# First weights by row block, squares a block late, and the memory rows' sums moved behind the index projections

## The chip, the core and the metric

The kernel runs on one NeuronCore of one Trainium2 chip. A core has five engines that run side by side, each through its own queue of instructions in a fixed order: TensorE (PE, matrix products; its weight loads are shown as PEld), VectorE (DVE), ScalarE (ACT), GpSimd (POOL) and SyncE (SP, which here issues the transfers between the chip's memory and the core's buffer). An instruction starts when it is at the head of its queue and what it waits for is done. The metric is the device time of one execution in microseconds; lower is better.

## What is computed

A decoder trunk of two layers over 512 tokens of width 1024, with five attention branches that share one normalised input, one of them attending to 256 memory rows. What matters here is the first projections of a layer and the memory branch:

```python
def _rmsnorm(x, g):
    xf = x.astype(jnp.float32)
    y = xf * lax.rsqrt(jnp.mean(xf * xf, axis=-1, keepdims=True) + EPS)
    return (y * g.astype(jnp.float32)).astype(x.dtype)

def _layer(x, mem, ...):
    h = _rmsnorm(x, norm_g)
    p = _split_columns(h @ w_in)
    ...
    y_c = _stick_breaking_attention(heads(p['sb_q']), heads(p['sb_k']), heads(p['sb_v']))
    ...
    mkv = _rmsnorm(mem, mem_norm) @ w_mem_kv
    mem_k = mkv[..., :BR_WIDTH].reshape(B, -1, N_HEADS, HEAD_DIM)
    mem_v = mkv[..., BR_WIDTH:].reshape(B, -1, N_HEADS, HEAD_DIM)
    y_e = _memory_attention(heads(p['mem_q']), mem_k, mem_v)
    ...
    return x + merged @ w_out
```

## The kernel before, in words

**Tiles.** Activations lie transposed: 1024 channels are 8 row blocks of 128 partitions, with 512 tokens along the free axis. Every float32 operand of a large product is split in two: a high part (ACT copies it into the rounded type) and a low part (DVE subtracts the high part from the original). `mm3` makes three products of each pair of blocks: high by high, low input by high weight, high input by low weight. A projection of 128 output columns (`proj`) is 8 row blocks times 3 = 24 matmuls.

**Weights.** `load` brings 128 x 1024 values (512 KB) through SP into one of two raw buffers (tag "raw", two of them), `split` turns them into `whi` and `wlo` (three buffers each). A raw buffer is free again when its low part is done, so SP's next weight transfer stands behind that. The memory rows (`mem_proj`, tile `mraw`) use the same two raw buffers.

**The start of layer 0.** `first` makes the projection of the first queries and keys (`sb_q`, `sb_k`, heads 0 and 1) from x that is multiplied by the norm's gain only; the row scale (root of the mean square) is applied to the results. `begin_tile` makes for each row block the high part `uh` (ACT), the square `sq` (ACT), the low part `ul` (DVE) and the running sum of squares (DVE). `inorder` writes the order on ACT and DVE out by hand: each instruction of the start stands behind the one before. The first weights come in two halves, one for each of the two output tiles (`START_W`), and are split behind row blocks 1 and 3. Then `sumsq` (PE adds the squares over channels), `rsqrt4` (twelve small steps on DVE, tiles `rs_v` to `rs_y`), `rotary_tables` (tile `ang`, then sine and cosine on ACT), the values of the first branch (`sb_v`), `rowb` (PE spreads the row scale over the partitions), and `norm`, which makes the normalised input `h_hi`, `h_lo` for all later projections.

**Behind it.** `memory_rows` makes the same root for the 256 memory rows: squares on ACT, sums on DVE (tile `sq`), the sum over channels on PE (`ssq`), the root on DVE, `rowb` on PE, and the result `rmem`. `sb_pair(1)` projects the second pair of queries and keys, `small_proj` the small heads and the index queries (`v2`, `iq`), `sb_attn` is the stick-breaking attention (tiles `sbz`, `sp_t`, `sp`, `sb_a`, and `Yc`, its product with the values). `mem_proj` scales the memory rows by `rmem` and the gain (`mraw`), splits them (`yhi`, `ylo`) and projects keys (`memk`, two tiles of 24 matmuls on 256 rows) and values (`memv`, 48).

**What sets the order.** A scheduler orders each engine's queue when the program is built, from the order of the code and the priorities; `weave` draws steps from generators in fixed shares, `chain` runs generators one behind the other, `take(g, n)` takes n steps, and `early` raises the priority of loads and splits.

Of the kernel before, what the change touches and what calls it, by code (L numbers as in the profile page):

```python
# [103 lines left out]
def _layout(x, mem, positions, norm_g, w_in, kv_norm, w_uk, w_uv, fox_bias, nsa_pe_k, nsa_pe_v,  # L104
# [6 lines left out]
    for l in range(L):  # L111
# [8 lines left out]
        for a, b in PAIRS:  # L120
            wall[l, CH[a]].reshape(128, 2, KT, 128)[:, 0] = cols(tl[a])
            wall[l, CH[a]].reshape(128, 2, KT, 128)[:, 1] = cols(tl[b])
# [64 lines left out]
def trunk(ctx: ExitStack, tc: tile.TileContext, xt, memt, pos, wall, small, vec, ca, cb, out):  # L187
# [27 lines left out]
    nc.scalar.preload_act_table_set("exp_and_others")  # L215
# [4 lines left out]
    START_W = (1, 3)  # L220
    start_w = []
    for k in range(KT):
        nc.sync.dma_start(xs[:, k], xt[:, k])
        if k in START_W:
            r = wts.tile([128, 1024], F32, name="wraw", tag="raw", bufs=2)
            nc.sync.dma_start(r, wall[0, CH[('sb_q', 0)], :, 1024 * len(start_w):1024 * len(start_w) + 1024])
            start_w.append(r)
# [147 lines left out]
    def memory_rows():  # L375
        rmem = const.tile([128, NM], F32, name="rmem")
        memp = [slot("memx", shape=(128, 2, NM)) for _ in range(4)]
        for j in range(4):
            nc.sync.dma_start(memp[j], memt[:, 2 * j:2 * j + 2])
        y = rsqrt4(sumsq([squares([memp[k // 2][:, k % 2] for k in range(KT)])], 2), D, 2)  # L380
        nc.scalar.activation(rmem, rowb(y, 2)[:, :NM], AF.Copy)
        tabs.rmem = rmem
        yield
# [288 lines left out]
    def begin_layer(l):  # L672

        U = [wk.tile([128, 2, T], F32R, name="u", tag=t, bufs=2) for t in ("yhi", "yhi", "ylo", "ylo", "Z", "Z")]
        u = [x[:, e] for x in U for e in range(2)]
        return SimpleNamespace(uh=u[:KT], ul=u[KT:] + [slot("ul", F32R) for _ in range(2 * KT - len(u))], sq=[])

    def begin_tile(b, l, k, x, inorder=lambda e, ins: ins, middle=lambda k: None):

        sq = slot("sq")  # L680
        g = vcol(l * V_L + V_NG + k)
        inorder(0, nc.scalar.activation(b.uh[k], x, AF.Copy, scale=g))
        middle(k)
        inorder(0, nc.scalar.activation(sq, x, AF.Square))
        inorder(1, nc.vector.scalar_tensor_tensor(b.ul[k], x, g, f32(b.uh[k]), op0=OP.mult, op1=OP.subtract))
        if k == 0 or (l and k == KT - 1):
            b.sq.append(sq)
        else:
            inorder(1, nc.vector.tensor_add(b.sq[0], b.sq[0], sq))

    def layer(l, xs, begin):
# [3 lines left out]
        def first():  # L695
# [4 lines left out]
            if l == 0:  # L700
# [5 lines left out]

                def start_split(k):
                    if k in START_W:
                        w = [wts.tile([128, 1024], F32R, name="w", tag=t, bufs=3) for t in ("whi", "wlo")]
                        r = start_w[START_W.index(k)]  # L710
                        inorder(0, nc.scalar.activation(w[0], r, AF.Copy))
                        inorder(1, nc.vector.tensor_sub(w[1], r, f32(w[0])))
                        ws.append(w)

                for k in range(KT):
                    begin_tile(b, 0, k, xs[:, k], inorder, start_split)
                state['start'] = prev[0], prev[1]
# [3 lines left out]
            for k in range(KT):  # L721
                for a in range(2):
                    c = slice(128 * k, 128 * k + 128)
                    mm3(p[a], ws[a][0][:, c], ws[a][1][:, c], uh[k], ul[k], k == 0, k == KT - 1)
# [661 lines left out]
        if l == 0:  # L1386
            run(chain(memory_rows(), take(sp1, 1)))
# [3 lines left out]
            weave((sb_attn(0), 8), (chain(silu2('sb_z', lv.ZC), take(ixp, 1), take(sp1, 1), take(ixp, 1), mp), 10))  # L1391
# [50 lines left out]
```

## Time and profile before

| | us |
|---|---|
| time, median of 3 executions | 1329.99 (1329.08 to 1330.47) |
| the profiled execution: time | 1330.9 |
| the profiled execution: span | 1329.1 |
| PE busy in the span | 1296.8 |
| DVE busy | 914.0 |
| ACT busy | 674.4 |
| first matmul starts | 9.31 |

The span reaches from the first to the last instruction of the profiled execution; 1.8 us lie around it. Busy time is what an engine spent in instructions; PE's ends are modelled, so a busy PE is not always at its peak rate. In the lists below "idle before <-X" names what ended the engine's wait.

### The profile page before, as it was taken

What the parts mean: (1) busy time and instruction counts of PE and PEld (TensorE: products, weight loads), DVE (VectorE), ACT (ScalarE), POOL (GpSimd) and SP (SyncE); (2) the same over time, 40 slices, a digit from 0 to 9 for tenths busy, and PEclk for the clock granted to TensorE, in tenths of its full rate; (3) what the DMA queues carried; (4) which work ended last, traced back from release to release, by engine and by line L of the source; (5) the groups of instructions that cost most, each with busy time, mean ns of one, the idle gap of its engine ahead of it and who ended that gap; (6) DMA issues with size and microseconds to landing.
All of it is one profiled execution on the core that took longest, in us unless ns stands there. A gap on an engine that the chain in (4) does not pass through costs nothing.

```text
span 1329.1 us, 18893 instructions
## 1 busy us (share of the span) xinstructions
PE 1296.8 (98%) x7160; PEld 1063.7 (80%) x7160; DVE 914.0 (69%) x1981; ACT 674.4 (51%) x1260; POOL 41.8 (3%) x60
## 2 busy tenths in 40 slices
PE   7999999999999999999999999999999999999997
PEld 6777777878888888888887777778788878888896
DVE  6887999768755546555567699995696564564554
ACT  6886835256545434334447695533574453343341
POOL 0000011000000000000000001110000000000000
PEclk9999999999999999999999999999999999999999
DMA  6432231312222222133523223222122222223231
GB/s 220 140 127 69 91 111 64 96 64 75 72 79 88 79 81 78 50 111 129 180 88 127 96 64 128 80 64 95 48 88 64 87 80 80 86 73 111 95 112 64
DMA packets 40235, 124.10 MB, mean 93 GB/s; under 512 B 4432, under 2 KB 6480, under 8 KB 40144
## 3 DMA queue, kind: packets, MB, share of 16 engines
q1 hardware_dynamic: 40144, 122.89, 28.6%
q8 instruction: 56, 0.92, 0.3%
q14 instruction: 35, 0.29, 0.1%
HBM read 118.16 MB, written 4.72 MB: 92 GB/s over the span
## 4 chain that ended last, share of the span: by engine, by line
PE 70%; DVE 6%; ACT 5%; issue 2%; DMA 1%; POOL 0%; DVEq 0%; ACTq 0%
PE pj L259 58%; PE Y L259 4%; PE S L259 3%; PE pt L556 3%; ACT whi L269 1%; DVE wlo L270 1%; DVE score L911 1%; DVE m L910 1%; DMA mraw<-in_memt_dram 1%; PE sbz L259 0%; ACT sw L431 0%; ACT sw L430 0%; ACT sp_t L388 0%; ACT Qi L854 0%; DVE rt L435 0%
## 5 line engine op out<-in xcount | busy, mean ns | idle before, releaser
L259 PE MATMUL pj<-h_hi,whi 128*128 128x512 f32 x1088 | 430.4, 397 | 1.3 <-DVE rt L433 1.0
L259 PE MATMUL pj<-h_lo,whi 128*128 128x512 f32 x1088 | 428.8, 394 | 0.0
L259 PE MATMUL pj<-h_hi,wlo 128*128 128x512 f32 x1088 | 427.9, 393 | 0.0
L269 ACT ACTIVATE whi<-wraw 128x1024 fp32r<-128x1024 f32 x183 | 193.4, 1057 | 347.1 <-PE pj L259 182.3
L270 DVE TENSOR_TENSOR wlo<-wraw,whi 128x1024 fp32r<-128x1024 f32 x183 | 223.6, 1223 | 197.8 <-ACT whi L269 178.7
L259 PEld LDWEIGHTS pj<-h_hi,wlo 128*128 128x128 f32 x1088 | 204.4, 188 | 44.5 <-DVE wlo L270 2.8
L259 PEld LDWEIGHTS pj<-h_hi,whi 128*128 128x128 f32 x1088 | 204.5, 188 | 43.5 <-issue 2.3
L259 PEld LDWEIGHTS pj<-h_lo,whi 128*128 128x128 f32 x1088 | 204.6, 188 | 41.6 <-issue 2.8
L547 ACT ACTIVATE P<-P,nm 128x128 f32<-128x128 f32 (+3 forms) x128 | 71.5, 559 | 55.5 <-DVE nm L546 54.7
L259 PE MATMUL pj<-yhi,whi 128*128 128x512 f32 (+1 forms) x192 | 72.2, 376 | 0.8 <-ACT whi L269 0.6
L259 PE MATMUL pj<-yhi,wlo 128*128 128x512 f32 (+1 forms) x192 | 71.6, 373 | 0.0
L259 PE MATMUL pj<-ylo,whi 128*128 128x512 f32 (+1 forms) x192 | 71.5, 373 | 0.0
L546 DVE CUSTOM_DVE_ANT_0 P<-S,CA 128x128 f32<-128x128 f32 (+3 forms) x104 | 48.0, 466 | 33.6 <-PE S L259 33.6
L556 PE MATMUL pt<-CA,P 128*128 128x128 f32 x384 | 60.7, 274 | 0.7 <-DVE P L595 0.5
L556 PEld LDWEIGHTS pt<-CA,P 128*128 128x128 f32 x384 | 45.6, 141 | 11.1 <-issue 3.6
L394 ACT ACTIVATE G<-pj 128x512 f32<-128x512 f32 x92 | 53.7, 583 | 0.3
L259 PE MATMUL S<-Ks,Qs 128*128 128x256 f32 (+2 forms) x160 | 50.0, 352 | 2.0 <-DVE nm L546 1.8
L911 DVE MATCH_REPLACE8 score<-m,score 128x256 f32<-128x256 f32 (+2 forms) x96 | 51.5, 541 | 0.0
L910 DVE MAX8 m<-score 128x8 f32<-128x256 f32 (+2 forms) x96 | 49.8, 547 | 0.0
L806 DVE TENSOR_TENSOR acc<-acc,G 128x512 f32<-128x512 f32 x64 | 44.0, 687 | 0.8
L805 DVE SCALAR_TENSOR_TENSOR G<-G,pj 128x512 f32<-128x512 f32 x64 | 43.6, 681 | 0.5 <-PE pj L259 0.2
L259 PEld LDWEIGHTS pj<-yhi,whi 128*128 128x128 f32 x192 | 36.1, 188 | 8.3 <-ACT whi L269 0.9
(326 smaller groups left out, 2028.5 us busy)
## 6 DMA issues: line engine op xcount, KB each, us to landing
wraw<-in_wall_dram SPq DMA_DIRECT2D x192, 512.0 KB, 3.7
wc<-in_wall_dram SPq DMA_DIRECT2D x16, 256.0 KB, 5.9
x<-in_xt_dram SPq DMA_DIRECT2D x8, 256.0 KB, 6.2
mraw<-in_memt_dram SPq DMA_DIRECT2D x4, 512.0 KB, 4.7
xo<-in_xt_dram SPq DMA_DIRECT2D x8, 256.0 KB, 3.8
xspill<-xn SPq DMA_DIRECT2D x8, 256.0 KB, 2.3
xo<-xspill SPq DMA_DIRECT2D x8, 256.0 KB, 3.2
out_dram<-o SPq DMA_DIRECT2D x8, 256.0 KB, 2.2
```

The source lines that it names most:

```text
L259: return nc.tensor.matmul(out_, lhsT, rhs, start=start, stop=stop, **kw)
L269: nc.scalar.activation(hi, raw, AF.Copy)
L270: nc.vector.tensor_sub(lo, raw, hi.bitcast(F32))
L394: i = nc.scalar.activation(*a, **k)
L546: nc.vector.tensor_tensor_reduce(P, S, mask, -1.0, 3e38, OP.add, OP.min, nm)
L547: nc.scalar.activation(P, P, AF.Exp, bias=nm, scale=-1.0, accum_out=sums)
L556: nc.tensor.transpose(pt[:, 128 * j:128 * j + 128], x[:, c:c + 128], ident)
L805: nc.vector.scalar_tensor_tensor(G, G, gc, p, op0=gop, op1=OP.mult)
L806: nc.vector.tensor_add(acc, acc, G)
L910: nc.vector.max(m8, lv.work[i])
L911: nc.vector.match_replace(lv.work[i], m8, lv.work[i], REPL)
```

## The change

**The start.** In layer 0 the weights of the first projection are laid out by row block: for each of the 8 row blocks the 128 columns of the queries and the 128 of the keys stand side by side. They are loaded in four pieces of two row blocks (128 x 512 values, 256 KB), the first one from ACT's queue ahead of its table load, the other three from SP's queue, each ahead of the two blocks of x that it belongs to. They are split piece by piece, ahead of the high part of every second row block. The squares run one row block late (`late_square`): behind the high and low part of block k stands the square of block k - 1. The projection's matmuls take their weights from the new places in both layers.

**The memory rows.** `memory_rows` yields behind the squares. Its first part stands behind the second queries instead of ahead of them; its second part (sum, root, `rmem`) stands in the long chain directly ahead of `mem_proj`.

```diff
@@ layout of the weights
+            w2 = wall[l, CH[a]].reshape(128, 2, KT, 128)
+            if a == ('sb_q', 0):
+                w2 = wall[l, CH[a]].reshape(128, KT, 2, 128).transpose(0, 2, 1, 3)
@@ loads of the start
-    nc.scalar.preload_act_table_set("exp_and_others")
...
-    START_W = (1, 3)
-    start_w = []
-    for k in range(KT):
-        nc.sync.dma_start(xs[:, k], xt[:, k])
-        if k in START_W:
-            r = wts.tile([128, 1024], F32, name="wraw", tag="raw", bufs=2)
-            nc.sync.dma_start(r, wall[0, CH[('sb_q', 0)], :, 1024 * len(start_w):1024 * len(start_w) + 1024])
-            start_w.append(r)
+    start_w = [wts.tile([128, 1024], F32, name="wraw", tag="raw", bufs=2) for _ in range(2)]
+
+    def start_load(k):
+        c = slice(512 * (k % 4) // 2, 512 * (k % 4) // 2 + 512)
+        nc.scalar.dma_start(start_w[k // 4][:, c], wall[0, CH[('sb_q', 0)], :, 256 * k:256 * k + 512])
+
+    start_load(0)
+    nc.sync.dma_start(xs[:, 0], xt[:, 0])
+    nc.sync.dma_start(xs[:, 1], xt[:, 1])
+    nc.scalar.preload_act_table_set("exp_and_others")
+    for k in range(2, KT, 2):
+        c = slice(512 * (k % 4) // 2, 512 * (k % 4) // 2 + 512)
+        nc.sync.dma_start(start_w[k // 4][:, c], wall[0, CH[('sb_q', 0)], :, 256 * k:256 * k + 512])
+        for e in range(2):
+            nc.sync.dma_start(xs[:, k + e], xt[:, k + e])
@@ memory_rows
-        y = rsqrt4(sumsq([squares([memp[k // 2][:, k % 2] for k in range(KT)])], 2), D, 2)
+        sq = squares([memp[k // 2][:, k % 2] for k in range(KT)])
+        yield
+        y = rsqrt4(sumsq([sq], 2), D, 2)
@@ begin_tile
+        middle(k)
         inorder(0, nc.scalar.activation(b.uh[k], x, AF.Copy, scale=g))
-        middle(k)
+        inorder(1, nc.vector.scalar_tensor_tensor(b.ul[k], x, g, f32(b.uh[k]), op0=OP.mult, op1=OP.subtract))
+        if l == 0:
+
+            b.rest.append((x, sq))
+            if k:
+                late_square(b, inorder)
+            return
         inorder(0, nc.scalar.activation(sq, x, AF.Square))
-        inorder(1, nc.vector.scalar_tensor_tensor(b.ul[k], x, g, f32(b.uh[k]), op0=OP.mult, op1=OP.subtract))
...
+    def late_square(b, inorder):
+        x, sq = b.rest.pop(0)
+        inorder(0, nc.scalar.activation(sq, x, AF.Square))
+        if b.sq:
+            inorder(1, nc.vector.tensor_add(b.sq[0], b.sq[0], sq))
+        else:
+            b.sq.append(sq)
@@ first
+                ws += [[wts.tile([128, 1024], F32R, name="w", tag=t, bufs=3) for t in ("whi", "wlo")] for _ in range(2)]
+
                 def start_split(k):
-                    if k in START_W:
-                        w = [wts.tile([128, 1024], F32R, name="w", tag=t, bufs=3) for t in ("whi", "wlo")]
-                        r = start_w[START_W.index(k)]
-                        inorder(0, nc.scalar.activation(w[0], r, AF.Copy))
-                        inorder(1, nc.vector.tensor_sub(w[1], r, f32(w[0])))
-                        ws.append(w)
+                    if k % 2 == 0:
+                        c = slice(256 * (k % 4), 256 * (k % 4) + 512)
+                        hi, lo = (x[:, c] for x in ws[k // 4])
+                        r = start_w[k // 4][:, c]
+                        inorder(0, nc.scalar.activation(hi, r, AF.Copy))
+                        inorder(1, nc.vector.tensor_sub(lo, r, f32(hi)))
...
-                    c = slice(128 * k, 128 * k + 128)
-                    mm3(p[a], ws[a][0][:, c], ws[a][1][:, c], uh[k], ul[k], k == 0, k == KT - 1)
+                    c = slice(256 * (k % 4) + 128 * a, 256 * (k % 4) + 128 * a + 128)
+                    mm3(p[a], ws[k // 4][0][:, c], ws[k // 4][1][:, c], uh[k], ul[k], k == 0, k == KT - 1)
@@ the body of layer
-            run(chain(memory_rows(), take(sp1, 1)))
+            mr = memory_rows()
+            run(chain(take(sp1, 1), take(mr, 1)))
...
-            weave((sb_attn(0), 8), (chain(silu2('sb_z', lv.ZC), take(ixp, 1), take(sp1, 1), take(ixp, 1), mp), 10))
+            weave((sb_attn(0), 8), (chain(silu2('sb_z', lv.ZC), take(ixp, 1), take(sp1, 1), take(ixp, 1), mr, mp), 10))
```

How the queues change is shown at three places. The first is DVE's queue at the start; before, its first rows were (`u<-x_79,VEC,u` is a low part of x, `w<-wraw,w` that of the weights, `sq<-sq` a sum of squares):

```order
L685 SCALAR_TENSOR_TENSOR u<-x_79,VEC,u 128x512
L712 TENSOR_TENSOR w<-wraw,w 128x1024
L685 SCALAR_TENSOR_TENSOR u<-x_79,VEC,u 128x512
L689 TENSOR_TENSOR sq<-sq 128x512
L685 SCALAR_TENSOR_TENSOR u<-x_79,VEC,u 128x512
L689 TENSOR_TENSOR sq<-sq 128x512
L712 TENSOR_TENSOR w<-wraw,w 128x1024
```

The weights' low parts stood between low parts of x, in two pieces. Now the same place on DVE reads:

```order
L741 TENSOR_TENSOR w<-wraw,w 128x512
L696 SCALAR_TENSOR_TENSOR u<-x_78,VEC,u 128x512 x2
L741 TENSOR_TENSOR w<-wraw,w 128x512
L696 SCALAR_TENSOR_TENSOR u<-x_78,VEC,u 128x512
L713 TENSOR_TENSOR sq<-sq 128x512
L696 SCALAR_TENSOR_TENSOR u<-x_78,VEC,u 128x512
L713 TENSOR_TENSOR sq<-sq 128x512
L741 TENSOR_TENSOR w<-wraw,w 128x512
```

A quarter of the weights stands ahead of each two blocks of x, and the sums begin behind the third low part. The second place is PE's queue behind the index queries' projection, whose last matmul is the first row here. Before (`smt_p` and `sw_p` belong to the small heads, `pj<-yhi,whi` is the first matmul of the memory keys):

```order
L259 MATMUL pj<-h_hi,wlo 128x512
L829 MATMUL smt_p<-CA,v_684 128x128 x4
L259 MATMUL sw_p<-v_684,CA 128x512
L259 MATMUL sbz<-Qs,Ks 128x256 x2
L259 LDWEIGHTS identb
L259 MATMUL sbz<-sbm,identb 128x256
L259 MATMUL sbz<-sp,nones 128x256 x4
L259 MATMUL sbz<-sp,nones 128x384 x2
L259 MATMUL sbz<-sp,ntri 128x512 x2
L259 MATMUL pj<-yhi,whi 128x256
```

The sum over the memory rows' channels (`ssq<-ones`) and the broadcast of their root (`rowb<-CA,rs_y`) had been done far ahead of this. Now PE's queue reads, from the last stick-breaking row of that piece on:

```order
L269 MATMUL sbz<-sp,ntri 128x512 x2
L269 MATMUL ssq<-ones_100,sq 128x1 x2
L269 MATMUL sbz<-Qs,Ks 128x384 x2
L269 LDWEIGHTS identb
L269 MATMUL sbz<-sbm,identb 128x128
L269 MATMUL sbz<-sp,ntri 128x256 x2
L269 MATMUL sbz<-Qs,Ks 128x256 x2
L269 LDWEIGHTS identb
L269 MATMUL sbz<-sbm,identb 128x256
L327 MATMUL rowb<-CA,rs_y 128x128 x2
```

Sum and broadcast came into this place, with stick-breaking products of the second head between them; the first matmul of the memory keys stands 13 rows behind the broadcast, and only stick-breaking rows are in between. The third place is SP's queue of transfers around the memory rows. Before (`memx` are the memory rows for the squares, `mraw` for the projection, `wraw` weights):

```order
L278 DMA wraw<-in_wall_dram 128x1024
L379 DMA memx<-in_memt_dram 128x512 x2
L1225 DMA mraw<-in_memt_dram 128x1024 x2
L251 DMA cbs<-in_cb_dram 128x512
L819 DMA cosI<-rot 128x1x512
L819 DMA sinI<-rot 128x1x512
L278 DMA wraw<-in_wall_dram 128x1024 x16
```

Two more `memx` stood ahead of the first row here. Now on SP:

```order
L288 DMA wraw<-in_wall_dram 128x1024 x4
L1254 DMA mraw<-in_memt_dram 128x1024
L389 DMA memx<-in_memt_dram 128x512 x4
L1254 DMA mraw<-in_memt_dram 128x1024
L261 DMA cbs<-in_cb_dram 128x512
L848 DMA cosI<-rot 128x1x512
L848 DMA sinI<-rot 128x1x512
L288 DMA wraw<-in_wall_dram 128x1024 x16
```

All four `memx` stand between the two `mraw` now; the weights of the memory projections (the first of the x16) stand behind both `mraw`, as before.

## Rows read from the trace of the kernel before

**Rows 1.** The profile's first part: busy us, share of span, instructions of each engine.
```profile
PE 1296.8 (98%) x7160; PEld 1063.7 (80%) x7160; DVE 914.0 (69%) x1981; ACT 674.4 (51%) x1260; POOL 41.8 (3%) x60
```

**Rows 2.** Windows: length, busy time (instructions) by engine, PEclk, DMA share, GB/s.
```profile
0.00:10.00 10.00, 0.69 (x2) 0.50 (x2) 1.55 (x4) 4.93 (x7) 0.20 (x4) 1.00 0.76 239
...
80.00:90.00 10.00, 8.81 (x67) 7.80 (x66) 9.15 (x17) 9.67 (x21) 0.00 (x0) 1.00 0.48 166
90.00:100.00 10.00, 8.95 (x59) 7.28 (x59) 7.67 (x12) 7.02 (x13) 0.00 (x0) 1.00 0.49 160
```

**Rows 3.** Timeline, start: us, duration, engine, line, out<-in xcount [idle before <-releaser].
```profile
4.28 0.72 ACT L682 ACTIVATE u<-x,VEC 128x512 fp32r<-128x512 f32 x1 [2.27 <-DMA x<-in_xt_dram]
...
8.21 1.06 ACT L711 ACTIVATE w<-wraw 128x1024 fp32r<-128x1024 f32 x1 [2.08 <-DMA wraw<-in_wall_dram]
...
9.29 1.23 DVE L712 TENSOR_TENSOR w<-wraw,w 128x1024 fp32r<-128x1024 f32 x1 [3.51 <-ACT w L711]
...
9.31 8.99 PE L259 MATMUL pj<-u,w 128*128 128x512 f32 x25 [9.31 <-ACT w L711]
...
14.10 0.74 DVE L685 SCALAR_TENSOR_TENSOR u<-x,VEC,u 128x512 fp32r<-128x512 f32 x1
...
14.77 0.68 DVE L689 TENSOR_TENSOR sq<-sq 128x512 f32<-128x512 f32 x1
...
15.37 0.75 DVE L685 SCALAR_TENSOR_TENSOR ul<-x,VEC,u 128x512 fp32r<-128x512 f32 x1
...
19.83 0.68 DVE L689 TENSOR_TENSOR sq<-sq 128x512 f32<-128x512 f32 x1
...
24.34 0.16 DVE L297 TENSOR_SCALAR rs_v<-ssq 128x4 f32<-128x4 f32 x1 [1.29 <-PE ssq L259]
...
27.01 0.43 DVE L364 TENSOR_SCALAR ang<-ang 128x512 f32<-128x512 f32 x1
```

**Rows 4.** Timeline, 30 to 50 us: the row scale's copy, and PE's wait.
```profile
31.48 0.60 ACT L347 ACTIVATE rb<-rowb 128x512 f32<-128x512 f32 x1
...
46.10 0.19 PEld L259 LDWEIGHTS pj<-h_lo,whi 128*128 128x128 f32 x1 [0.22 <-DVE h_lo L270]
```

**Rows 5.** Timelines of PE (first row) and DVE: the memory rows and forget gates.
```profile
59.13 0.61 PE L259 MATMUL ssq<-ones,sq 128*128 128x1 f32 x4 [0.38 <-DVE sq L342]
...
60.06 0.16 DVE L297 TENSOR_SCALAR rs_v<-ssq 128x2 f32<-128x2 f32 x1
...
64.06 0.48 DVE L1228 SCALAR_TENSOR_TENSOR mraw<-mraw,VEC,rmem 128x256 f32<-128x256 f32 x1
...
70.05 0.74 DVE L270 TENSOR_TENSOR ylo<-mraw,yhi 128x256 fp32r<-128x256 f32 x2
...
80.92 0.69 DVE L882 SCALAR_TENSOR_TENSOR fu<-fu,fe 32x512 f32<-32x512 f32 x1 [0.21 <-ACT fe L388]
```

**Rows 6.** Timelines of SP and ACT: the first memory weights, issue and split.
```profile
70.52 0.34 SPq L278 DMA_DIRECT2D wraw<-in_wall_dram  x1
...
74.22 1.06 ACT L269 ACTIVATE whi<-wraw 128x1024 fp32r<-128x1024 f32 x1 [0.52 <-DMA wraw<-in_wall_dram]
```

**Rows 7.** Timeline of PE, 74 to 101 us: index queries' end, memory keys, Yc.
```profile
74.52 0.40 PE L259 MATMUL pj<-h_hi,wlo 128*128 128x512 f32 x1
74.75 0.60 PE L829 MATMUL smt_p<-CA,v 128*128 128x128 f32 x4
...
77.71 0.28 PE L259 MATMUL pj<-yhi,whi 128*128 128x256 f32 x1
...
80.47 0.28 PE L259 MATMUL pj<-yhi,wlo 128*128 128x256 f32 x1
...
98.85 2.38 PE L259 MATMUL Yc<-sb_a,VC 128*64 128x512 f32 x16 [0.71 <-ACT sb_a L388]
```

**Rows 8.** Windows near the end, columns as in rows 2.
```profile
1320.00:1322.00 2.00, 0.00 (x0) 0.00 (x0) 1.65 (x11) 0.00 (x0) 0.00 (x0) 1.00 0.00 0
...
1324.00:1326.00 2.00, 0.00 (x0) 0.00 (x0) 2.00 (x6) 0.00 (x0) 0.00 (x0) 0.50 0.66 218
```

More of the change, by code (lines that the diff above doesn't have):

```diff
@@ L120, in _layout @@
         for a, b in PAIRS:
-            wall[l, CH[a]].reshape(128, 2, KT, 128)[:, 0] = cols(tl[a])
-            wall[l, CH[a]].reshape(128, 2, KT, 128)[:, 1] = cols(tl[b])
+            w2 = wall[l, CH[a]].reshape(128, 2, KT, 128)
+            if a == ('sb_q', 0):
+                w2 = wall[l, CH[a]].reshape(128, KT, 2, 128).transpose(0, 2, 1, 3)
+            w2[:, 0] = cols(tl[a])
+            w2[:, 1] = cols(tl[b])
         for n in VTOK:
@@ L675, in begin_layer @@
         u = [x[:, e] for x in U for e in range(2)]
-        return SimpleNamespace(uh=u[:KT], ul=u[KT:] + [slot("ul", F32R) for _ in range(2 * KT - len(u))], sq=[])
+        return SimpleNamespace(uh=u[:KT], ul=u[KT:] + [slot("ul", F32R) for _ in range(2 * KT - len(u))], sq=[], rest=[])
     def begin_tile(b, l, k, x, inorder=lambda e, ins: ins, middle=lambda k: None):
@@ L681, in begin_tile @@
         g = vcol(l * V_L + V_NG + k)
+        middle(k)
         inorder(0, nc.scalar.activation(b.uh[k], x, AF.Copy, scale=g))
-        middle(k)
+        inorder(1, nc.vector.scalar_tensor_tensor(b.ul[k], x, g, f32(b.uh[k]), op0=OP.mult, op1=OP.subtract))
[4 more added lines that the diff above has]
+            return
         inorder(0, nc.scalar.activation(sq, x, AF.Square))
-        inorder(1, nc.vector.scalar_tensor_tensor(b.ul[k], x, g, f32(b.uh[k]), op0=OP.mult, op1=OP.subtract))
-        if k == 0 or (l and k == KT - 1):
+        if k == 0 or k == KT - 1:
             b.sq.append(sq)
@@ L705, in inorder @@
                     prev[e] = ins
+                ws += [[wts.tile([128, 1024], F32R, name="w", tag=t, bufs=3) for t in ("whi", "wlo")] for _ in range(2)]
                 def start_split(k):
-                    if k in START_W:
-                        w = [wts.tile([128, 1024], F32R, name="w", tag=t, bufs=3) for t in ("whi", "wlo")]
-                        r = start_w[START_W.index(k)]
-                        inorder(0, nc.scalar.activation(w[0], r, AF.Copy))
-                        inorder(1, nc.vector.tensor_sub(w[1], r, f32(w[0])))
-                        ws.append(w)
+                    if k % 2 == 0:
[4 more added lines that the diff above has]
+                        inorder(1, nc.vector.tensor_sub(lo, r, f32(hi)))
                 for k in range(KT):
                     begin_tile(b, 0, k, xs[:, k], inorder, start_split)
+                late_square(b, inorder)
                 state['start'] = prev[0], prev[1]
```

## The prediction

> **What bounds the kernel now.** I read the share of busy time first: PE is busy for 98% of the span [rows 1], so time can only be won where PE stands idle, and any new idle time of PE is paid in full. The windows say where PE is idle early: 9.3 us before its first matmul, and 2.2 us between 80 and 100 us [rows 2]. The timeline of the start says why: the first matmul waits for ACT's split of the first weights at 8.21, and that for a 512 KB transfer [rows 3]. From 9.29 to 20.51 (19.83 + 0.68) DVE runs without a pause [rows 3]. At 46.10 PE waits for DVE's low parts of the normalised input [rows 4]. So PE's late start is one limit of the first 46 us and DVE's queue is the other. Last I read the stage from 74 us on, where memory keys and values are projected [rows 5 to 7].
>
> **The change: the start.** The weights of the first projection come in four 256 KB pieces, one for two row blocks, instead of two halves, one for each output tile. The first piece goes out on ACT's queue. No row shows a transfer issued by ACT. The nearest is SP's first block of x, of the same size, in use at 4.28 [rows 3], so the piece lands at about 4.2. ACT's table load now stands behind that issue; ACT had 2.27 us of waiting for x behind it, so it stays hidden. PE can then start at about 5.1 instead of 9.31, but it can't use that alone. Each block needs DVE's low part, and DVE's work is, from start to start, 0.67 for a low part, 0.60 for a sum of squares (14.10, 14.77, 15.37) and about 1.16 for a 1024-column weight split [rows 3]: 2 x 1.16 + 7 x 0.67 + 7 x 0.60 = 11.2, the measured stretch. Now it is 4 x 0.60 + 8 x 0.67 + 7 x 0.60 = 12.0. If DVE never waited it would run from 4.8 to 16.8, 3.7 us earlier. But transfers arrive in turn: the first weight half, with 1.1 MB up to its end, was in use at 8.21 [rows 3], and 1.1 MB now end with the second weight piece. DVE gets its fifth operation at 8.2 + 0.6 = 8.8, with 3 x 0.6 + 6 x 0.67 + 7 x 0.60 = 10.0 to go: the sums end at 18.8 instead of 20.51. I take 1.7, since the row that it rests on is the same engine's wait for the same bytes; the ends are 0 and 3.7.
>
> What follows on DVE is nearly the same list up to the clamp of the angles at 27.01. DVE waited 1.29 of it for PE's sum [rows 3], now about 0.3, but both low parts of the next weights now stand behind that sum, so PE, early as it is, waits for them. ACT's queue goes absolute value, table load, sine, cosine, and now a weight split, which stood ahead of this chain, before it writes the row scale at 31.48 [rows 3, 4]: 1.06 us [rows 6] added to a path of 4.0 us. DVE then needs one weight split more ahead of the first scaled row. Clamp 2.2 us earlier, less about 0.9 for these, leaves **1.3 us** at the point where PE waited at 46.10 [rows 4]. Ends: 0 and 3.5.
>
> **The change: the memory rows.** Before, their squares, sum, root and row scale were done between 52 and 64 us under two projections; what PE pays there is a wait of 0.38 for the sum, the sum's 0.47 [rows 5], and about 0.25 for the broadcast. That is 1.1 us that leave this place and come back behind the projection of the index queries. That projection ends in before at E = 74.52 + 0.23 = 74.75 [rows 7]; after, at 74.75 - 1.3 - 1.1 = 72.35. The squares stay hidden, as their DVE and ACT work is as long as before and lies under projections.
>
> The order shows what is late next. PE's queue has the sum behind all that stood ahead of the memory keys before, so 2.96 us after E (77.71 - 74.75) [rows 7]. From there it is one chain with nothing large left on PE:
> - sum to DVE's first step 0.93 (59.13 to 60.06): E + 3.9 [rows 5].
> - root, broadcast, scale, to the first scaled memory row: 60.06 to 64.06 is 4.0 [rows 5]. A gate product that stood between drops out; a cast, a subtraction and two steps of the forget gates now stand there, the longest 0.69 (80.92) [rows 5]; I add 1.3 for the exchange: 5.3, so E + 9.2.
> - The memory rows hold both buffers for raw weights, so SP issues the next weights only when the fourth low part is done. Six scalings and four low parts at 0.40 (two took 0.74 at 70.05) [rows 5]: 4.0, so E + 13.2. Before it took 6.4, with other work between; that is the upper end.
> - transfer 3.7 (70.52 to 74.22), split 1.06 [rows 6], low part 1.23 (a split of that size, 9.29) [rows 3], behind 0.7 of stick-breaking steps: E + 19.9.
> - the first key tile's other 22 matmuls at 0.12 (24 between 77.71 and 80.47) [rows 7]: E + 22.5. The second tile, 24: E + 25.4. For the values' second weight half the low part two loads earlier must be done, at about E + 22.6; 3.7 + 1.06 + 1.23 behind it is E + 28.6, and 34 matmuls, 4.1: E + 32.7. The values' product with the attention weights, Yc, 2.3: **E + 35.0**.
>
> Before, Yc ended at 98.85 + 2.3 = 101.2 [rows 7], with seven matmuls of the next projection, at 0.23, already done: worth 99.55, E + 24.8. So the stage is 10.2 us longer, and against the clock it ends at 107.35 instead of 99.55. The cover is gone because the projections that hid the chain are all ahead of it. Nothing behind gives it back: all other engines' queues are in the same order, and PE is 98% busy over the span [rows 1].
>
> **Sum.** -1.3 - 1.1 + 10.2 = +7.8 us. The profiled execution took 1330.9 (span 1329.1); the median of the three runs is 1330.0, so I put the time at 1330.0 + 7.8, rounded 1338.
>
> **Rivals.** (a) *Hidden and faster.* DVE never waits at the start (3.7 kept) and the memory chain finds cover: 1326.3. For it: PE is idle 9.3 us at the start [rows 2]. Against: it needs the root to be finished within the 2.96 us of PE work behind E, where 4.0 us alone were measured for it [rows 5]. It decides only if the sum stood ahead of the last projection, and the order shows it behind. (b) *No change.* The memory weights don't wait for the buffers (two buffers free early): PE then starts the keys at about E + 10.8 with the first low part, ends the first tile at 17, runs the rest without a pause to 26.4, Yc to 28.7: +3.9 - 2.4 = +1.5, 1331.5. Against: before, SP issued the next weights at 70.52, just when the fourth low part (second of 70.05) was done [rows 5, 6]. (c) *The clock falls.* PE stands still for some 6 us before the memory keys. In the tail of before the granted clock is 1.00 in a window in which PE did nothing, and 0.50, the lower level of 1.2 GHz, in one that begins 4 us later, with hardly any matmul between [rows 8]. Then the first tile's 24 matmuls take 0.24 instead of 0.12, 2.9 us, and up to 2.9 more come from the next: 1341 to 1344. Against: part of it falls into waits for weights; I keep 0.3 of it at the forecast's high end. The Trainium skill ("TensorE: Matmul & The Clock Gate", Part 1) says that half rate is the default and that activity releases it; by that the first matmuls at 9.31 would be slow, while the window 0 to 10 here has a granted clock of 1.00 [rows 2], so the page and the start differ, and the tail agrees with it.
> (d) *The start brings nothing,* because 256 KB pieces land later: the gain of 1.3 turns into 0, 1339.3; this lies within the range.
>
> **How the numbers follow.** Forecast, with (d) inside: 0.72. Clock: 0.12. No change: 0.08. Faster: 0.08. The forecast's own range: gain 3.5 instead of 1.3 and a chain 2.5 shorter (low parts and scalings side by side) is 1338 - 4.7 = 1333; the fourth low part after 6.4 instead of 4.0, no gain at the start and 0.3 of the clock is 1338 + 2.4 + 1.3 + 0.3 = 1342. To leave out no more than 2 in 10 the range takes in case (b) and the lower half of (c): 1331 to 1343. Differences under 0.2% (2.7 us) can't be told from no change here. Faster 0.08, same 0.08, slower 0.84.
>
> **What would show it.** Right: first matmul near 5; DVE's sums end near 19; the PE wait before the row of 46.10 ends 1 to 2 us earlier; a new PE wait of several us around 80 to 92, put down to ACT's split of the memory weights, whose transfer is issued right after the fourth low part of the memory rows; Yc ending near 107. Wrong: memory keys on PE within 5 us of E, or a front part that ends by more than 4 us earlier.

## The result, and the profile after

The changed kernel takes 1340.2 us (median of four executions, 1339.8 to 1341.0) where the kernel before, measured beside it, takes 1330.2 (1329.1 to 1330.5): a ratio of 1.0074, 95% interval 1.0062 to 1.0086. That is 10.0 us or 0.74% slower, in the direction and within the range that were forecast, and 2.2 us above the forecast's 1338.0. Its profiled execution took 1339.8 with a span of 1338.0; against the profiled execution of before that is 8.9 us, and the traces explain 8.8 of them (1.0 won in front, 9.8 lost in the memory stage). The other 1.1 is the place of the two profiled executions among the others.

The page first, its line of busy times [rows 1]; then the windows of the changed kernel, where the columns are the stretch, its length, the busy time of PE, PEld, DVE, ACT and POOL with the number of instructions, the granted clock of PE, the share of the transfers and GB/s [rows 2]:

```profile
PE 1300.9 (97%) x7160; PEld 1067.1 (80%) x7160; DVE 914.9 (68%) x1983; ACT 675.5 (50%) x1262; POOL 41.9 (3%) x60
```

```profile
0.00:10.00 10.00, 3.94 (x9) 2.76 (x9) 3.93 (x8) 6.19 (x10) 0.20 (x4) 1.00 0.74 241
...
20.00:30.00 10.00, 8.53 (x72) 8.32 (x72) 5.87 (x18) 4.79 (x8) 0.00 (x0) 1.00 0.42 135
...
80.00:90.00 10.00, 3.57 (x12) 2.45 (x12) 9.68 (x25) 7.57 (x21) 0.00 (x0) 0.50 0.18 52
90.00:100.00 10.00, 9.91 (x65) 9.41 (x66) 7.58 (x14) 6.27 (x11) 0.00 (x0) 0.83 0.48 158
```

PE gained 3.25 us in the first window and lost 5.2 between 80 and 90, where DVE is the busy engine and PE's clock stands at its lower level. The next list has the waits of PE up to 130 us, each with its releaser, total, count and longest:

```profile
PE pj L269 <- ACT u L695: 6.1, 1, 6.1
PE sbz L269 <- DVE sp_t L996: 5.0, 1, 5.0
PE rowb L327 <- DVE rs_y L319: 1.9, 1, 1.9
PE pj L269 <- DVE w L765: 1.5, 1, 1.5
PE sbz L269 <- ACT sbm L263: 1.2, 1, 1.2
PE pj L269 <- ACT whi L279: 0.7, 1, 0.7
PE sbz L269 <- ACT sb_a L400: 0.4, 1, 0.4
```

They add up to 16.8 us; before they were 9.3 at the start and six of 0.7 or less, 12.1. So waits grew by 4.7 and busy time by 4.1 [rows 1], for the same 7160 matmuls: a slow matmul counts as busy for longer (0.63 us instead of 0.39 for 128 x 512, rows of e1 below). The new waits are the root of the memory rows (`rs_y`), DVE's stick-breaking steps that stand behind the memory rows (`sp_t`), the low parts of the next weights (`w`) and the mask constants (`sbm`).

The start of the changed kernel, ACT, PE and DVE in the timeline (start, length, what; in brackets the idle time before and what ended it) [rows 3]:

```profile
4.35 0.63 ACT L740 ACTIVATE w<-wraw 128x512 fp32r<-128x512 f32 x1 [1.91 <-DMA wraw<-in_wall_dram]
5.29 1.34 ACT L695 ACTIVATE u<-x,VEC 128x512 fp32r<-128x512 f32 x2 [0.31 <-DMA x<-in_xt_dram]
```

```profile
6.06 8.73 PE L269 MATMUL pj<-u,w 128*128 128x512 f32 x25 [6.06 <-ACT u L695]
19.84 0.95 PE L269 MATMUL ssq<-ones,sq 128*128 128x1 f32 x8
22.84 1.57 PE L269 MATMUL pj<-w,u 128*128 128x256 f32 x11 [1.47 <-DVE w L765]
```

```profile
17.16 1.48 DVE L713 TENSOR_TENSOR sq<-sq 128x512 f32<-128x512 f32 x2
...
20.82 0.16 DVE L307 TENSOR_SCALAR rs_v<-ssq 128x4 f32<-128x4 f32 x1 [1.39 <-PE ssq L269]
...
25.38 0.43 DVE L374 TENSOR_SCALAR ang<-ang 128x512 f32<-128x512 f32 x1
```

And the memory stage, PE, DVE, SP and ACT in the order of time [rows 5 to 7]:

```profile
73.75 0.60 PE L858 MATMUL smt_p<-CA,v 128*128 128x128 f32 x4
...
76.71 0.50 PE L269 MATMUL ssq<-ones,sq 128*128 128x1 f32 x4
...
81.44 0.69 PE L327 MATMUL rowb<-CA,rs_y 128*128 128x128 f32 x2 [1.87 <-DVE rs_y L319]
...
88.77 0.80 PE L269 MATMUL sbz<-sp,nones 128*128 128x256 f32 x2 [4.99 <-DVE sp_t L996]
...
93.56 0.28 PE L269 MATMUL pj<-yhi,wlo 128*128 128x256 f32 x1
...
106.09 2.38 PE L269 MATMUL Yc<-sb_a,VC 128*64 128x512 f32 x16
```

```profile
82.67 1.28 DVE L1257 SCALAR_TENSOR_TENSOR mraw<-mraw,VEC,rmem 128x256 f32<-128x256 f32 x3
...
86.17 0.42 DVE L280 TENSOR_TENSOR ylo<-mraw,yhi 128x256 fp32r<-128x256 f32 x1
...
91.52 1.23 DVE L280 TENSOR_TENSOR wlo<-wraw,whi 128x1024 fp32r<-128x1024 f32 x1
```

```profile
86.61 13.24 SPq L288 DMA_DIRECT2D wraw<-in_wall_dram  x5
```

```profile
90.43 1.06 ACT L279 ACTIVATE whi<-wraw 128x1024 fp32r<-128x1024 f32 x1 [0.18 <-DMA wraw<-in_wall_dram]
```

This is the forecast chain: the fourth low part ends at 86.59 (86.17 + 0.42), SP issues the key weights at 86.61, ACT splits them at 90.43, DVE's low part ends at 92.75, PE goes on with the keys at 93.56.

### The profile page after: what moved, and what is told of

Read it like the earlier page. It is cut to its first block, busy times and chain, and to the rows that moved or that the text cites. A ratio compares the mean times of both kernels' runs of the same rounds, so it can differ in the third digit from the quotient of the medians.

```text
span 1338.0 us, 18910 instructions
## 1 busy us (share of the span) xinstructions
PE 1300.9 (97%) x7160; PEld 1067.1 (80%) x7160; DVE 914.9 (68%) x1983; ACT 675.5 (50%) x1262; POOL 41.9 (3%) x60
## 4 chain that ended last, share of the span: by engine, by line
PE 79%; ACT 8%; DVE 8%; issue 3%; DMA 2%; POOL 0%; SPq 0%; DVEq 0%; ACTq 0%; POOLq 0%
PE pj L269 65%; PE Y L269 4%; PE S L269 4%; PE pt L568 3%; ACT whi L279 2%; DVE wlo L280 1%; PE sbz L269 1%; ACT sw L443 1%; ACT sw L442 1%; ACT sp_t L400 1%; DVE score L940 1%; DVE m L939 1%; DMA mraw<-in_memt_dram 1%; DMA wraw<-in_wall_dram 1%; ACT Qs L477 1%
## 5 line engine op out<-in xcount | busy, mean ns | idle before, releaser
L1305 POOL TENSOR_SCALAR P<-P,rsum 128x256 f32<-128x256 f32 x32 | 30.9, 978 | 372.3 <-ACT Ks L498 223.3
```

The source lines that it names most:

```text
L1305: nc.gpsimd.tensor_scalar(x, x, r[:, e:e + 1], None, op0=OP.mult)
```

## The experiments

The experiments were timed in five rounds, each against the kernel before on the same chip; its medians there were 1330.1 to 1330.6. The changed kernel's row is the measurement above. The ratios are to the kernel before, with their 95% intervals; where two intervals overlap, the two kernels can't be told apart by time. Each trace shows one execution.

| run | us | ratio |
|---|---|---|
| changed kernel | 1340.2 | 1.0074 (1.0062 to 1.0086) |
| e1, start only | 1334.0 | 1.0030 (1.0019 to 1.0041) |
| e2, memory rows only | 1339.2 | 1.0068 (1.0055 to 1.0081) |
| e3, rows in own tiles | 1335.1 | 1.0035 (1.0021 to 1.0048) |
| e4, root three ahead | 1337.4 | 1.0051 (1.0039 to 1.0064) |
| e5, constants first | 1342.3 | 1.0093 (1.0080 to 1.0106) |
| e6, root one ahead | 1338.7 | 1.0067 (1.0055 to 1.0079) |
| e7, start, sum held | 1336.6 | 1.0051 (1.0039 to 1.0064) |
| e8, the same and two edits | 1336.2 | 1.0045 (1.0033 to 1.0058) |
| e9, sum only | 1339.1 | 1.0066 (1.0054 to 1.0078) |
| e10, front order | 1338.5 | 1.0061 (1.0049 to 1.0073) |
| e11, tiles, root, front | 1329.4 | 0.9991 (0.9982 to 1.0000) |
| e12, root two ahead | 1329.3 | 0.9993 (0.9984 to 1.0002) |

### The two halves of the change apart: e1, e2, e9

e1 takes the changed kernel and puts the memory rows back; e2 takes the kernel before and moves them:

```diff
@@ e1
-            mr = memory_rows()
-            run(chain(take(sp1, 1), take(mr, 1)))
+            run(chain(memory_rows(), take(sp1, 1)))
...
-            weave(... take(ixp, 1), mr, mp), 10))
+            weave(... take(ixp, 1), mp), 10))
@@ e2: the reverse, on the kernel before, with the yield in memory_rows
```

> The changed start alone; the memory rows as in the kernel before. Theory: in the changed kernel the normalised input's low parts come about 1.0 us earlier than before, and nothing later in this kernel takes that back: 1329.2 (1328.5 to 1329.7), with the sum of squares on PE 3.5 us earlier than before and the first key tile of the memory rows about 1 us earlier. Rival one, the 3.5 us won at the sum of squares survive and only the moved memory rows used them up: 1326.7. Rival two, the new start brings nothing or costs: 1330.2 or more.

> The moved memory rows alone; the start as in the kernel before. Theory: the stage behind the index queries' projection grows by the 9.8 us that the changed kernel shows, 1.1 us of PE work and waiting for the memory rows' sum leave the earlier place, and a wait of 1.2 us for the mask constants comes in: 1340.1 (1339 to 1341). If the two parts of the change help each other (the rows' root has more cover when the start is not early) it would be 1337 or less; if the start has a loss of its own hidden in the total, it is the changed kernel's 1340.2 minus that loss.

e2 came out 0.9 below its theory's 1340.1, inside its range. e1 refuted my theory and the first rival. The second, "brings nothing or costs", held, but had no size and no cause: alone, the new start costs 4 us. PE of e1:

```profile
54.71 0.61 PE L269 MATMUL ssq<-ones,sq 128*128 128x1 f32 x4 [2.03 <-DVE sq L352]
57.61 0.52 PE L269 MATMUL pj<-h_hi,whi 128*128 128x512 f32 x1 [2.29 <-DVE Qs L470]
57.92 0.63 PE L269 MATMUL pj<-h_lo,whi 128*128 128x512 f32 x1
58.35 0.63 PE L269 MATMUL pj<-h_hi,wlo 128*128 128x512 f32 x1
...
61.92 0.39 PE L269 MATMUL pj<-h_hi,wlo 128*128 128x512 f32 x1
```

DVE of e1:

```profile
50.42 3.06 DVE L352 TENSOR_TENSOR sq<-sq 128x256 f32<-128x256 f32 x6
53.52 0.68 DVE L470 SCALAR_TENSOR_TENSOR Qs<-pj,Qs 64x512 fp32r<-64x512 f32 x1
```

With the other start the scheduler put the memory rows' sum behind 72 matmuls of the projections in PE's queue, where it had stood behind 94. DVE has six sums of squares in a row ahead of the queries' low part, and PE waits for the sums (2.03) and then for that low part (2.29), and then runs at its lower level: one matmul takes 0.63 instead of 0.39 until 61.1, and 0.43 us from start to start instead of 0.23. So the halves don't add: 4.0 and 9.1 apart, 10.0 together. Given the moved memory rows, the new start is worth nothing that can be told: 1340.2 with it, 1339.2 without, the intervals overlap.

e9 moves the sum, root and row scale alone (with the yield in `memory_rows`, as in e2); squares and start stay as before:

```diff
-            run(chain(memory_rows(), take(sp1, 1)))
+            mr = memory_rows()
+            run(chain(take(mr, 1), take(sp1, 1)))
...
-            weave(... take(ixp, 1), mp), 10))
+            weave(... take(ixp, 1), mr, mp), 10))
```

> The kernel before with the second part of the memory rows alone (sum over channels, root, row scale) moved directly ahead of the memory keys; start and squares stand as before. Theory: the late sum is the whole loss of the moved memory rows: 1339 (1338 to 1340.5), with the keys' weights issued right behind the fourth low part of the memory rows. Rival, the late squares (their transfers crowd the mask constants' and weights') carry a good part: 1336 or less.

The theory held. PE's waits of e9, and SP's issue of the key weights:

```profile
PE sbz L259 <- DVE sp_t L969: 5.7, 1, 5.7
PE rowb L317 <- DVE rs_y L309: 1.9, 1, 1.9
```

```profile
87.42 12.86 SPq L278 DMA_DIRECT2D wraw<-in_wall_dram  x5
```

The same two waits, the same late issue, the same 9 us (1.0066, e2 1.0068): the late sum is the whole loss, and the place of the squares adds nothing to it that can be told.

### What the late sum holds up: e3

In the first layer the memory rows are scaled in the tiles of their squares, so that they don't sit in the raw weight buffers and aren't loaded twice:

```diff
+                if l:
+                    mx_ = wts.tile([128, 4, NM], F32, name="mraw", tag="raw", bufs=2)
+                    nc.sync.dma_start(mx_, memt[:, 4 * j:4 * j + 4])
...
+                    x = mx_[:, i] if l else tabs.memp[k // 2][:, k % 2]
...
```

> The changed kernel, but in the first layer the memory rows are scaled in the tiles that their squares were made from, and are not loaded a second time into the two raw weight buffers. Theory: the raw buffers are free, so the key weights are there before the rows; the first key tile follows the rows' low parts (ended 15.4 us behind the index queries' projection in the changed kernel), values and their product end at 26 to 28 us behind it instead of 34.6: 1333 (1331 to 1335), with SP's next weight transfer issued tens of us earlier. Rival, the root's own length and the half clock make the stage long and the buffers don't matter: 1338 or more.

1335.1, at the upper end of the theory's range. Free raw buffers give back 5.1 of the 10.0 us. The next weights are issued at 63.62 instead of 86.61. What stays is the root: PE waits 2.5 us for its last step and 1.6 for a stick-breaking step, starts the keys at 87.00 and makes the first of them at the lower clock (0.50 from 80.10 to 90.34). PE of e3 at two places of the key projection, 0.21 and 0.12 us from start to start:

```profile
88.24 0.42 PE L269 MATMUL pj<-yhi,whi 128*128 128x256 f32 x1
88.45 0.41 PE L269 MATMUL pj<-ylo,whi 128*128 128x256 f32 x1
...
92.03 0.28 PE L269 MATMUL pj<-yhi,wlo 128*128 128x256 f32 x1
92.15 0.28 PE L269 MATMUL pj<-yhi,whi 128*128 128x256 f32 x1
```

### The sum at other places: e4, e6, e7

e4 draws `mr` in the chain three projections earlier, e6 one earlier, everything else as in the changed kernel. e7 has the squares ahead of the second queries, as before, and holds the sum behind the small heads (`state["pj"]` is the last matmul of the projection drawn last):

```diff
@@ e4
+ chain(silu2('sb_z', lv.ZC), mr, take(ixp, 1), take(sp1, 1), take(ixp, 1), mp)
@@ e6
+ chain(silu2('sb_z', lv.ZC), take(ixp, 1), take(sp1, 1), mr, take(ixp, 1), mp)
@@ e7
+            run(chain(take(mr, 1), take(sp1, 1)))
...
+        y = rsqrt4(sumsq([sq], 2, state["pj"]), D, 2)
+ chain(silu2('sb_z', lv.ZC), take(ixp, 1), mr, take(sp1, 1), take(ixp, 1), mp)
```

> The changed kernel with the second part of the memory rows (sum over channels, root, row scale) drawn three projections earlier, behind the first gate's projections and ahead of the small heads, the second keys and the index queries. Theory: the whole chain of root, scaling and weights then lies under about 17 us of projections, and the stage has its old length: 1340.2 - 9.8 = 1330.4, or up to 1 us below (1329.2 to 1330.8). Rival, the stage's length comes from the late squares and the queue of DVE and not from the place of the sum: 1336 or more.

> The changed kernel with the second part of the memory rows (sum, root, row scale) drawn one projection earlier, behind the second keys and ahead of the index queries. Theory: the root's chain gets the 24 matmuls of the index queries as cover, 24 x 0.23 = 5.5 us, and the memory rows' squares are done by then, so PE does not wait for them as it did with the root three projections earlier (2.0 us there): 1340.2 - 5.5 = 1334.7 (1333.5 to 1336). Rival, each earlier place only moves the wait to the squares: 1337 or more.

> The changed start, with the memory rows' squares ahead of the second queries as in the kernel before, and the sum over channels held in PE's queue behind the small heads' projection (96 of the projections' matmuls ahead of it; 94 in the kernel before, 72 where the start was changed alone). Theory: the changed start alone cost 4 us because it moved this sum 22 matmuls forward in PE's queue, onto data that was not there (PE waited 2.0 and 2.3 us, and ran at a lower clock behind that); with the sum held where it was, the new start costs nothing and keeps about 1 us: 1329.2 (1328.3 to 1330.2). Rival, the start itself costs the 4 us: 1334.

All three theories fell. e4 gave back 2.8 us: PE waits 2.0 for the squares' sums, as its rival had it. Its profiled execution, the slowest of five, has another 1.4 us of loss at the start that the sum's place has nothing to do with (last section). e6 gave back 1.5 of 5.5, and its interval overlaps that of the changed kernel; its time is the rival's, its cause is not, for PE has no wait for the squares there. The key weights are still issued only when the fourth low part is done (78.24), PE waits 3.1 for `sp_t`, 1.9 for the mask constants and 1.2 for low parts of weights. e7 has no wait for the sum, as its theory said, but in its place PE waits longer for the queries, and the kernel is slower than the rival's 1334 as well:

```profile
PE pj L269 <- DVE Qs L470: 3.7, 1, 3.7
```

DVE still does six sums of squares ahead of the low part that frees the projection's bank. So it wasn't the sum's place alone that made the new start dear in e1, but DVE's order there. The change's move of the squares behind the second queries takes this wait away; the changed kernel, e4 and e6, which all have it, show no such wait: in the changed kernel the seven sums start at 58.79, behind both low parts.

### The front: e5, e10, e8

e5 issues the mask constants ahead of the memory rows; e10 splits the first half of the next weights on DVE ahead of the first root; e8 is e7 with both:

```diff
@@ e5
+            cbs = load_constants()
             run(chain(take(sp1, 1), take(mr, 1)))
@@ e10
+            ss = sumsq(b.sq, 4)
+            if l == 0:
+                value_weights(0)
+            y = rsqrt4(ss, D, 4)
```

> The changed kernel with the transfer of the mask constants (cbs) issued ahead of the memory rows' five transfers instead of behind them; the tail from the index queries on stands as in the changed kernel. Theory: in the changed kernel PE waits 1.2 us at 62 us for these constants, at the same moment as with the old start, so the wait swallows what the new start had won; with the constants early the wait goes and the whole time falls by 1.0 to 1.2: 1339.0 to 1339.2. Rival, the start's lead is lost elsewhere (PE must wait for DVE or for weights in that place anyway): 1340.2.

> The changed kernel with the low part of the first half of the next weights (sb_v) ahead of the first root's steps in DVE's queue, where DVE waits 1.4 us for PE's sum. In the run that had this edit among others, stick-breaking began on PE 1.56 us earlier than in a run with as late a start without it (45.46 and 47.02). Theory: an earlier front is worth nothing to the end of this kernel, since PE then waits as much longer for the mask constants at 62 us: 1340 (1339.3 to 1340.8), with that wait at 2.5 us or more. Rival, the lead reaches the end: 1338.7.

> As the kernel with the sum held behind the small heads, and two edits more: the mask constants are loaded ahead of the memory rows, and the first half of the next weights (sb_v) is split on DVE ahead of the first root's steps, in the time in which DVE waits for PE's sum (1.4 us in the changed kernel). Theory: PE's wait of 1.5 us for these weights shrinks and the angles' clamp comes 1.1 us earlier: 1328 (1326.8 to 1329.2), below both kernels. Rival, DVE's queue is full behind 30 us and gives the time back at the normalised input: 1329.2 to 1330.

e5 was wrong in sign: with the constants early, the scheduler takes the stick-breaking matmuls earlier, PE waits 2.1 us for a DVE step (`sp`) there, and the kernel is 2 us slower by its median, though the two intervals overlap by a little. e10's theory fell by its trace: the wait for the constants is 1.02 and not 2.5 or more. Its time, 1338.5, is the rival's, but the interval overlaps that of the changed kernel. PE of e10:

```profile
44.84 0.29 PE L269 MATMUL sbz<-Qs,Ks 128*128 128x256 f32 x1
...
60.74 0.38 PE L269 MATMUL sbz<-sbm,identb 128*128 128x256 bf16 x3 [1.02 <-ACT sbm L263]
...
71.97 0.60 PE L867 MATMUL smt_p<-CA,v 128*128 128x128 f32 x4
```

Stick-breaking starts 1.65 us earlier than in the changed kernel (46.49), the index queries' projection ends 1.78 earlier (71.97), the profiled execution is 2.3 shorter. The order makes this lead and not a lucky start, since the first sum on PE begins at 20.12 there, later than the changed kernel's 19.84. In these two traces the lead of the front reaches the end. e8 missed its theory of 1328 by 8 us and can't be told from e7 (1336.2 and 1336.6): its front is early too (45.46), but a bank wait of 4.6 us for DVE swallows the lead.

### Putting the findings together: e11, e12

e11 is e3, e6 and e10 in one; e12 holds the sum of e11 one projection earlier.

> Three edits of the changed kernel at once: the memory rows scaled in their squares' tiles (1335.1 alone), the root one projection earlier (1338.7 alone) and the front order on DVE. Theory: with the raw buffers free, what was left of the stage was the root's 4 us and PE's lower clock behind its waits, and the index queries' projection covers that: 1335.1 - 4 - 1 = 1330 (1328 to 1332), no better than the kernel before. Rival, the gains don't add since the wait for the stick-breaking steps on DVE takes their place: 1334 or more.

> As the kernel with the memory rows in their squares' tiles and the front order, but with the sum held behind the small heads' projection, one projection earlier still (ahead of the second keys). In the kernel before this one PE still waited 2.3 us for the memory rows' low parts (two waits) and the squares' sums on DVE ended at 60.25, where PE was at about 60 us. Theory: the sum finds its squares done (wait under 0.6 us), the rows' low parts come some 5 us earlier, and the 2.3 us go: 1329.4 - 2.3 + 0.5 = 1327.6 (1326.5 to 1328.8), below the kernel before. Rival, the wait moves to the squares and to DVE's stick-breaking steps: 1329.4 or more.

PE's waits of e11 after the start, without those of 0.2, are down to these:

```profile
PE pj L269 <- DVE ylo L280: 2.3, 2, 1.6
PE sbz L269 <- ACT sbm L263: 0.6, 1, 0.6
```

The 10.0 us are gone, as the theory had it. The gains more than add: alone the three edits gave 5.1, 1.5 and 1.7, 8.3 in all, and together they give 10.8. The traces of e6 and e3 fit that: with the root early the key weights still waited for a raw buffer, and with free buffers the root was still late, so that each edit left the other's limit standing. At 1329.4 and 1329.3 the kernels stand 1 us under the one before, which can't be told from no change. e12's theory fell: the two waits shrink to one of 1.0, but PE waits 2.2 for the squares' sums.

## Why the prediction was right, and where not

**The memory stage, +10.2, was right: +9.8.** The stage counts from E, the end of the index queries, now at 73.75:

| step | forecast | measured |
|---|---|---|
| DVE's first root step | E + 3.9 | E + 3.7 (77.41) |
| first scaled memory row | E + 9.2 | E + 8.9 (82.67) |
| fourth low part, next transfer issued | E + 13.2 | E + 12.8 (86.59) |
| key weights' low part done | E + 19.9 | E + 19.0 (92.75) |
| first key tile done | E + 22.5 | E + 22.4 |
| second key tile done | E + 25.4 | E + 25.3 |
| values done | E + 32.7 | E + 32.3 |
| Yc done | E + 35.0 | E + 34.6 (108.39) |

Against E + 24.8 that is 9.8 us. Nearly every price came from a row of before, and the exchange that was guessed (1.3 us of forget-gate steps in the root's path) was within 0.1. The close agreement from the first key tile on is in part luck: the low part of the key weights was done 0.9 earlier than forecast, mainly because the 0.7 of stick-breaking steps did not stand in its way (ACT's split ends at 91.49, DVE starts at 91.52), and PE went on 0.8 later than that, held up by slow stick-breaking matmuls that the chain did not have. The two misses cancel. e9 shows by itself that the sum's place makes the loss, e3 that the raw buffers hold half of it, as the chain has it from the fourth low part to the key weights.

**The two terms in front, −1.3 and −1.1, were too large together: −1.0 at E instead of −2.4.** At the start the steps went in the forecast direction. The first matmul came at 6.06 and not near 5.1, DVE's sums ended at 18.64 (18.8 forecast), the clamp came 1.6 us earlier (2.2), stick-breaking starts 0.9 earlier (46.49, before 47.37). Two waits were not seen.

The first is DVE's wait for PE's sum. The prediction put it at "about 0.3" without a working; it was 1.39 (the row of 20.82 above). PE came to the sum only at 19.84, and its first matmuls ran at the lower level of its clock. PE of the changed kernel between 7 and 11 us, and between 13 and 19 (count, busy us, mean ns):

```profile
L269 PE MATMUL pj<-u,w 128*128 128x512 f32 x10 | 4.6, 644 | 0.0
```

```profile
L269 PE MATMUL pj<-u,w 128*128 128x512 f32 x21 | 6.1, 390 | 0.0
```

These are the durations of the two levels in e1 (0.63 and 0.39); in the kernel before the mean is 648 ns between 11 and 15 us. The 1.00 that the window rows give for 0 to 10 us, before [rows 2] and after, is not a measurement: the traces hold no entry for the clock ahead of 15.28 (before) and 11.53 (after), where it is at its upper level, and the view fills that with 1.00. So the prediction misread this row where it says that the start and the page differ: the matmuls' durations agree with what it tells of the Trainium skill there. PE did nothing before its first matmul (6.06) and worked from there until the clock rose (11.53). In e6, with the same start, the clock rose at 9.57, and with DVE's sums ended at 18.78 PE began its sum at 18.92. DVE of e6:

```profile
19.92 0.16 DVE L307 TENSOR_SCALAR rs_v<-ssq 128x4 f32<-128x4 f32 x1 [0.35 <-PE ssq L269]
```

The wait is the forecast's 0.3 there, and the clamp comes at 24.48, 2.5 earlier than in the kernel before and 0.9 earlier than in the changed one. That is what the clock's later rise cost by this pair of traces; no run changes the clock alone.

The second is PE's wait of 1.2 us for the mask constants. ACT of the kernel before, then ACT and PE of the changed one:

```profile
61.73 0.42 ACT L253 ACTIVATE sbm<-cbs 128x256 bf16<-128x256 f32 x1 [0.79 <-DMA cbs<-in_cb_dram]
```

```profile
62.06 0.42 ACT L263 ACTIVATE sbm<-cbs 128x256 bf16<-128x256 f32 x1 [0.87 <-DMA cbs<-in_cb_dram]
```

```profile
62.53 0.38 PE L269 MATMUL sbz<-sbm,identb 128*128 128x256 bf16 x3 [1.18 <-ACT sbm L263]
```

The constants stand behind 2 MB of memory rows in SP's queue, and were there at about 62 us in both kernels. In the kernel before, PE came just then (62.20, no wait); now it comes earlier and waits. This is the step that failed: the front's gain and the 1.1 us of the memory rows' sum were booked as kept, without asking for what arrives at that place next. e2, with the old start, has the same E (73.67), though its stick-breaking starts later (46.98), so at E the new start's share is next to nothing. That is the number of case (d), 1339.3, but not its reason: the pieces did not land too late for the forecast sums.

**The rivals.** (a) needs the sum ahead of the last projection; e4 and e6 put it there and won only 2.8 and 1.5 us, because the squares and the raw buffers are the next limits: that rival's single condition was not enough (e6's 1.5 can't be told from nothing). (b), free buffers, was priced at 1331.5; e3 made them free and gave 1335.1, so that price was 3.6 too low: E came 0.6 earlier than before and not 2.4, the keys started 12.9 us behind E (87.00, E at 74.12) instead of 10.8, and at the lower clock. (c), the clock, fell as described (0.50 and 0.83), but it hardly paid: PE goes on 0.8 us after the weights' low part (93.56 and 92.75), and the broadcast takes 0.69 where e9's, at the same place, takes 0.43. That is about 1 us, read from the trace and not tried by itself. Two other traces give about half: in e9 and e10 the lower level lasts 10.2 us there instead of 13.7, and the stage ends 34.1 us behind E instead of 34.6. The 0.3 kept for it was small.

**After the stage nothing is given back,** as forecast: the second layer's first small-heads transposes come 8.4 us later than before, the end 8.9.

**Marks.** The wait put down to ACT's split of the key weights did not appear in that form: PE's wait between 83.8 and 88.77 is put down to DVE's `sp_t`, since stick-breaking matmuls stand ahead of the keys; behind them slow matmuls fill the time until the weights are there. The place and the length were right, the name was not.

## What to carry to other kernels

Before a sum moves behind its last cover, count what its result releases: here a root of 12 small DVE steps was cheap, but it held eight scalings, two weight buffers and every transfer behind them. When work leaves a place, ask what arrives there next; here 1.2 us of the gain ended at the next late arrival, though PE was busy 98%. Where a scheduler sets the order, look at the order after each edit: with a start that is 1 us faster it put a sum 22 matmuls further forward and a row of sums ahead of the queries, and the kernel lost 4 us. And take a clock from the matmuls' durations where the trace has no entry for it.

## What was not expected of the hardware

**Behind the same wait at the start the clock was lower in some traces and not in others.** In the changed kernel PE waits 1.47 us for the next weights and goes on at 1.00 (the row of 22.84 above: 11 matmuls in 1.57). e1, e3, e5 and e6 do the same. In e4, whose queues hold the same instructions up to there, the 11 take 2.72; e3's row is the first, e4's the second:

```profile
23.33 1.58 PE L269 MATMUL pj<-w,u 128*128 128x256 f32 x11 [1.48 <-DVE w L766]
```

```profile
23.35 2.72 PE L269 MATMUL pj<-w,u 128*128 128x256 f32 x11 [1.48 <-DVE w L765]
```

```profile
20.00:30.00 10.00, 8.52 (x57) 8.08 (x56) 6.82 (x21) 4.88 (x7) 0.00 (x0) 0.83 0.39 113
```

The window is e4's; e7 shows 0.83 there too (2.34). e3 and e4 come to this place at the same time, and stick-breaking starts at 47.02 and 48.43; e7 and the changed kernel do (22.87 and 22.84), and it starts at 47.98 and 46.49. So the lower level costs 1.4 to 1.5 us here, more than the new start had won. Why the clock fell only in e4 and e7 is open. e10's order removes this wait, and its clock stays at 1.00.

**A transfer on a second queue delays the first one on the other.** With a 256 KB piece of weights on ACT's queue, the first block of x, issued by SP at the same 1.18 as before, is in use at 5.29 instead of 4.28 (5.11 to 5.49 in the eleven traces with the new start, in six of which ACT still waits for it then; 4.27 to 4.34 in the three with the old one). This is part of why the first matmul came at 6.06. The Trainium skill ("DMA: Bandwidth & Descriptors", "Queues, rings and completion order") says that each transfer engine takes turns between the queues that have work for it; the delay agrees with that, though no row here shows the turns themselves.

**The start varies more with the new start, as far as one trace of each kernel tells.** In the eleven kernels that have it, the first sum of squares on PE begins between 18.6 and 20.3 us; in the three with the old start between 23.0 and 23.4. Two things differ between the eleven: when the second piece of weights lands (ACT splits it at 7.58 in the changed kernel, at 9.06 in e4 behind a wait of 1.83 for the transfer) and when PE's clock rises (9.17 to 12.28).

What stays open is why the mask constants arrive no earlier with the new start (their issue moves by 0.2 us against e2, while e10's moves by 1.6). The traces answer a part: SP issues them behind the second `mraw`, and that one waits for a raw buffer. It goes out at 55.56, when a low part of weights is done (54.30 + 1.23 = 55.53), so the constants too hang on these buffers. An earlier one of these low parts starts at 48.25 in the changed kernel and at 48.04 in e2, in spite of the earlier front, because DVE's queue has both low parts of the keys ahead of it (46.45 and 47.29) where e2's has one (47.01). From issue to ACT's cast the constants take between 5.2 us (before) and 6.8 (e6), and that difference stays unexplained.
